# Differential attention in a hybrid encoder: one joint maximum over all keys for both softmax components, and the small VectorE operations in another order

## The chip, the cores and the metric

The kernel runs on one core of a Trainium2 chip. The metric is the device time of one execution in microseconds (us); the time before is a median of three runs. One further view, the trace, comes from a profiled execution and gives start and duration of each instruction on each engine: TensorE (PE, with its weight loads PEld), VectorE (DVE), ScalarE (ACT), GpSimd (POOL) and SyncE (SP).

## The reference, cut to what matters

Two layers; each has an input projection, two gated scans, a differential attention over 2048 positions, and an output projection. The change lies in the attention. For each of 4 heads and each block of 128 queries:

```
def block(qblk):
    s = jnp.einsum('cbhqd,cbhkd->cbhqk', qblk, k).astype(jnp.float32)   # c: 2 components, 2048 keys
    p = jax.nn.softmax(s, axis=-1)
    w = p[0] - lam * p[1]
    return jnp.einsum('bhqk,bhkv->bhqv', w.astype(v.dtype), v)
o = rms_norm(o, norm_w) * (1.0 - lambda_init)
```

The result of a block is normalised afterwards, so the kernel computes e0 - lam * (sum0 / sum1) * e1 from the exponentials and sums of the two components, and gives the square of sum0 to the norm's epsilon.

## The kernel before, in words

A layer's attention is swept in 64 units (4 heads x 16 blocks of 128 queries). A unit has four tiles of scores s0 to s3, each 128 queries x 1024 keys in two PSUM banks: s0 and s1 are the two halves of the keys for component 0, s2 and s3 for component 1. The loop over f advances one tile per step; step f works on tile `f % 4` of unit `f // 4`, and on older units at fixed lags. In what follows "position 0 to 3" is f % 4, and a prime marks the next unit (s0' follows s3).

The order on PE, DVE, ACT and POOL is written out by hand (`manual_schedule`): each engine executes its instructions in the order in which the loop's lines issue them, and only the transfers on SP are placed by a planner. In each step PE does the scores (4 matmuls), then `values` of an older unit, then `transposes` of another. DVE does the row maxima of the tile and the combination e0 + factor * e1 of half a unit at positions 0 and 2. ACT copies the transposed weights out of PSUM (`copy`), then does its exponentials (`exps`), and at position 0 also `save`, which empties the output bank `po` before `values` of the next unit may begin at position 1. At lag 1 of every eighth step ACT has one more instruction between `copy` and `exps`, `fetch`: every second unit from unit 16 to 46 PE computes at position 3 a product for the scans (`poi`, 12 matmuls ahead of s3), and `fetch` takes it out of PSUM at position 0 of the unit after.

PSUM is full: s tiles and `poi` together have three double-bank buffers, dealt out by a counter that all their allocations share, and by `acc`, which the projections call 148 times in a layer ahead of its attention. Two of three turns take one of two buffers of pool "b" (whichever is free first), the third takes the only one of pool "t":

```
        turn[0] += 1
        key, bufs = (("b", 2), ("b", 2), ("t", 1))[turn[0] % 3]
        return psum[key][1].tile([P, 2, 512], F32, tag="two", name=name, bufs=bufs)
```

A layer's attention takes 272 turns (256 s and 16 poi) and the output projection 16. Two single banks remain: one holds `po` over four steps, the other the transposed weights `pt`.

Before the change component 0 has one maximum over both halves (`mx[:, 4]`, the smaller of two negated maxima), and its two exponentials run together at position 2. Component 1 has a maximum for each half: the exponential of s2 runs at position 3 and that of s3 at position 0 of the next unit, each as soon as its own maximum is there. Two weights (`weights`, L929) and their corrections (`lows`, `total`, `factors`) bring the halves together later, so that `combine` has a factor for each half.

On POOL, the scan states (L768, L771) run beside the first units of a layer, the normalisation of the scans' output (L825 to L838) beside the middle units, and the splitting of the output weights (L785, L787) beside the later ones; the casts of queries (L723, L725) and the gates (L943, L944) run throughout.

Of the kernel before, what the change touches and what calls it, by code (L numbers as in the profile page):

```python
# [11 lines left out]
F32 = mybir.dt.float32  # L12
# [3 lines left out]
AF = mybir.ActivationFunctionType  # L16
ALU = mybir.AluOpType
AX = mybir.AxisListType
# [3 lines left out]
P = 128  # L22
# [28 lines left out]
EPS = 1e-6  # L51
# [9 lines left out]
def tile_hybrid_encoder(  # L61
# [9 lines left out]
    nc = tc.nc  # L71
# [168 lines left out]
    for l in range(DEPTH):  # L240
# [12 lines left out]
        if l == 0:  # L253
            h_st, hhi, hlo, npre = open_h(0)
            w_st, w_first = open_w(0)
# [488 lines left out]
            psum_close("s")  # L744
            psum_open("b", f"psb{l}", "left")

# [1 line left out]
        with ExitStack() as s2:  # L748
            at = at_st.enter_context(tc.tile_pool(name=f"at{l}", bufs=1, side="left"))
            si_st = ExitStack()  # L750
# [12 lines left out]
            for i in range(14):  # L763
                for d in range(2):
                    c, sh = (i + 1, 1) if d == 0 else (14 - i, -1)
# [74 lines left out]
                    nc.sync.dma_start(dr_y[self.r, 768:1024], oi[:, 256:512])  # L840

            class Unit:
                """One block of 128 queries of one head; s counts its tiles of scores (component, half of the keys)."""

                def __init__(self, i):
                    self.h, self.qb = divmod(i, NT)
                    self.j = self.qb % 2
                    if self.j == 0:
                        if (self.h, self.qb // 2) not in qs_of:
                            load_q(self.h, self.qb // 2)  # L850
                    self.qh, self.ql, self.ga = qs_of[self.h, self.qb // 2]
                    self.ks, self.v = kv[self.h]
                    self.mx = at.tile([P, 6], F32, tag="mx", name="mx", bufs=4)
                    self.sm = at.tile([P, 4], F32, tag="sm", name="sm", bufs=4)
                    self.gm = at.tile([P, 10], F32, tag="gam", name="gam", bufs=4)
                    self.s, self.pt, self.wt = [None] * 4, [None] * 4, [None] * 4

                def scores(self, k):
# [8 lines left out]
                        nc.tensor.matmul(s[:, i], self.ql[:, c, js], kk, start=False, stop=True)  # L867

                def maxima(self, k):
                    mx = self.mx  # L870
                    nc.vector.tensor_reduce(mx[:, k:k + 1], self.s[k].rearrange("p a n -> p (a n)"), axis=AX.X, op=ALU.max,  # L871
                                            negate=True)
                    if k == 1:
                        nc.vector.tensor_tensor(mx[:, 4:5], mx[:, 0:1], mx[:, 1:2], op=ALU.min)

                def exps(self, k):
                    for kk in ((), (0, 1), (2,), (3,))[k]:
                        c, n = divmod(kk, 2)
                        m = 4 if c == 0 else kk
                        nc.scalar.activation(self.es[c][:, n * 1024:(n + 1) * 1024], self.s[kk].rearrange("p a n -> p (a n)"),  # L880
                                             AF.Exp, bias=self.mx[:, m:m + 1], accum_out=self.sm[:, kk:kk + 1])

                def lows(self):
                    nc.vector.tensor_tensor(self.mx[:, 5:6], self.mx[:, 2:3], self.mx[:, 3:4], op=ALU.min)

                def sums(self):
                    gm, sm = self.gm, self.sm
                    nc.vector.tensor_tensor(gm[:, 2:3], sm[:, 0:1], sm[:, 1:2], op=ALU.add)

                def sums2(self):  # L890
                    gm = self.gm
                    nc.vector.tensor_scalar(gm[:, 1:2], gm[:, 2:3], neglam, None, op0=ALU.mult)
                    nc.vector.tensor_scalar(gm[:, 3:4], gm[:, 2:3], EPS, gm[:, 2:3], op0=ALU.mult, op1=ALU.mult)

                def total(self):
                    gm, sm = self.gm, self.sm
                    nc.vector.scalar_tensor_tensor(gm[:, 6:8], gm[:, 4:6], 1.0, sm[:, 2:4], op0=ALU.mult, op1=ALU.mult,
                                                   accum_out=gm[:, 0:1])

                def inverse(self):  # L900
                    nc.vector.reciprocal(self.gm[:, 0:1], self.gm[:, 0:1])

                def factors(self):
                    gm = self.gm
                    nc.vector.tensor_scalar(gm[:, 8:10], gm[:, 4:6], gm[:, 0:1], gm[:, 1:2], op0=ALU.mult, op1=ALU.mult)

                def combine(self, n):
                    es, gm, hs = self.es, self.gm, slice(n * 1024, (n + 1) * 1024)
                    nc.vector.scalar_tensor_tensor(es[0][:, hs], es[1][:, hs], gm[:, 8 + n:9 + n], es[0][:, hs],  # L909
                                                   op0=ALU.mult, op1=ALU.add)  # L910

                def transposes(self, q):
# [8 lines left out]
                def values(self, q):  # L921
                    if q == 0:
                        self.po = one_bank([P, P], "po", "t")
                    for i in range(4):
                        k = 4 * q + i
                        nc.tensor.matmul(self.po, self.wt[q][:, i], self.v[:, k], start=k == 0, stop=k == NT - 1)  # L926

                def weights(self):
                    nc.scalar.activation(self.gm[:, 4:6], self.mx[:, 2:4], AF.Exp, scale=-1.0, bias=self.mx[:, 5:6])  # L929

                def save(self):
                    self.o = at.tile([P, P], F32, tag="o", name="o", bufs=2)
# [16 lines left out]
            with tc.manual_schedule(engines={getattr(mybir.EngineType, e) for e in ENGINES}):  # L949
                for f in range(4 * NU + 13):  # L950
# [7 lines left out]
                    def at_lag(lag, name, k=None, *args):  # L958
                        i, m = divmod(f - lag, 4)
                        if 0 <= i < NU and k in (None, m):  # L960
                            getattr(units[i], name)(*((m,) if k is None else args))

                    def inter(lag, name):
                        c, k = divmod(f - lag - 4 * I0 - 3, 4 * I_STEP)
                        if k == 0 and 0 <= c < NT:
                            if name is None:
                                inters[c] = Inter(c)
                            else:
                                getattr(inters[c], name)()
# [3 lines left out]
                    at_lag(0, "scores")  # L973
                    at_lag(9, "values")
                    at_lag(7, "transposes")
                    at_lag(4, "lows", 0)
                    at_lag(6, "combine", 0, 0)
                    at_lag(6, "combine", 2, 1)
                    at_lag(5, "total", 0)
                    at_lag(3, "sums", 0)  # L980
                    at_lag(0, "maxima")
                    at_lag(5, "inverse", 0)
                    at_lag(3, "sums2", 0)
                    at_lag(5, "factors", 0)
                    at_lag(8, "copy")
                    inter(1, "fetch")
                    at_lag(1, "exps")
                    at_lag(4, "weights", 0)
                    at_lag(10, "norm", 3)
                    at_lag(9, "save", 3)  # L990
                    inter(2, "square")
# [129 lines left out]
```

## Time and profile before

| | |
|---|---|
| median of 3 runs | 3755.73 us |
| lowest, highest run | 3752.49, 3758.89 us |
| span of the profiled execution, first to last instruction | 3752.0 us |
| PE, PEld busy | 94%, 85% of the span |
| DVE, ACT, POOL busy | 72%, 59%, 50% of the span |
| attention of layer 0, of layer 1 | about 1034 to 1675 us, 2905 to 3550 us |

The page gives no separate time for the profiled execution; its span lies 0.5 us under the lowest run. The shares are means over stages with different limits, so the attention has to be read by its own stretches.

### The profile page before, as it was taken

The numbers are of one execution on the slowest core, as the hardware profiler recorded it, in microseconds if no ns is written. First come the engines' busy times: TensorE is split into PE (matmuls) and PEld (weight loads), VectorE is DVE, ScalarE is ACT, GpSimd is POOL, SyncE is SP. The second block draws the span as 40 slices with busy tenths as digits, with TensorE's granted clock in tenths as the row PEclk, the third lists the DMA queues.
The fourth block names the chain that finished last, engine by engine and source line by source line (L and its number), as shares of the span: only waits on it lengthen the run. The fifth ranks groups of instructions, "written<-read, shape, count | busy, mean of one in ns | idle before, by whom it ended". The sixth has DMA issues, their size and how long they took to land.

```text
span 3752.0 us, 62823 instructions
## 1 busy us (share of the span) xinstructions
PE 3534.9 (94%) x22976; PEld 3175.5 (85%) x22976; DVE 2691.2 (72%) x4122; ACT 2203.1 (59%) x5140; POOL 1868.5 (50%) x1854
## 2 busy tenths in 40 slices
PE   8999989988989999899999999999889899998999
PEld 7898978877978999788888989889779789997887
DVE  5422789988499999985324238898784999999733
ACT  4521577755568888774225125776555778887722
POOL 3545655565576666520035455555555756664200
PEclk9999999999999999999999999999999999999999
DMA  4443444444441332214334444444444413322133
GB/s 156 133 136 128 134 129 138 137 123 135 131 136 33 117 119 85 66 32 133 120 115 150 125 127 136 129 137 140 126 126 132 126 39 117 115 79 66 38 134 114
DMA packets 293652, 430.54 MB, mean 115 GB/s; under 512 B 42400, under 2 KB 185312, under 8 KB 291040
## 3 DMA queue, kind: packets, MB, share of 16 engines
q1 hardware_dynamic: 268896, 333.71, 28.7%
q0 software_dynamic: 22336, 90.71, 8.3%
q8 instruction: 182, 2.98, 0.3%
q10 hardware_dynamic: 2112, 2.10, 0.2%
q14 instruction: 126, 1.03, 0.1%
HBM read 275.82 MB, written 152.57 MB: 114 GB/s over the span
## 4 chain that ended last, share of the span: by engine, by line
PE 51%; DVE 27%; DMA 10%; issue 4%; POOL 4%; ACT 3%; SPq 1%; DVEq 0%; POOLq 0%; ACTq 0%
PE pp L306 11%; PE pob L1031 9%; PE po L926 8%; PE pp L297 6%; DVE mx L871 5%; PE s L866 4%; PE s L867 4%; PE pt L915 4%; DMA wraw<-in_w_in_dram 3%; DVE e L909 3%; DVE qt L612 3%; DVE pr L545 3%; DVE att L605 2%; DMA cs<-c_rope 2%; PE poi L816 1%
## 5 line engine op out<-in xcount | busy, mean ns | idle before, releaser
L880 ACT ACTIVATE e<-s,mx 128x1024 f32<-128x1024 f32 x512 | 570.5, 1118 | 146.6 <-DVE mx L871 107.3
L871 DVE TENSOR_REDUCE mx<-s 128x1 f32<-128x1024 f32 x512 | 621.3, 1215 | 36.7 <-PE s L867 35.9
L306 PE MATMUL pp<-wlo,hhi 128*128 128x256 f32 (+1 forms) x2048 | 591.0, 289 | 7.8 <-POOL wlo L224 7.7
L926 PEld LDWEIGHTS po<-vt,wt 128*128 128x128 f32 x4096 | 533.2, 191 | 70.0 <-ACT o L933 30.0
L306 PE MATMUL pp<-whi,hlo 128*128 128x256 f32 (+1 forms) x2048 | 591.8, 289 | 0.1
L306 PE MATMUL pp<-whi,hhi 128*128 128x256 f32 (+1 forms) x2048 | 588.0, 287 | 3.0 <-DVE whi L223 3.0
L926 PE MATMUL po<-vt,wt 128*128 128x128 f32 x4096 | 544.1, 276 | 17.4 <-ACT o L933 17.4
L866 PE MATMUL s<-ks,aqh 128*128 128x512 f32 x1024 | 449.7, 439 | 28.0 <-ACT e L880 26.5
L297 PE MATMUL pp<-hhi,whi 128*128 128x512 f32 x1024 | 412.1, 402 | 3.7 <-DVE zg L428 2.4
L297 PE MATMUL pp<-hhi,wlo 128*128 128x512 f32 x1024 | 410.1, 400 | 0.0
L297 PE MATMUL pp<-hlo,whi 128*128 128x512 f32 x1024 | 410.0, 400 | 0.0
L867 PE MATMUL s<-ks,aql 128*128 128x512 f32 x1024 | 404.0, 395 | 5.2 <-POOL aql L725 5.2
L306 PEld LDWEIGHTS pp<-wlo,hhi 128*128 128x128 f32 x2048 | 393.1, 192 | 8.8 <-POOL wlo L224 8.8
L306 PEld LDWEIGHTS pp<-whi,hhi 128*128 128x128 f32 x2048 | 395.0, 193 | 4.1 <-DVE whi L223 3.8
L306 PEld LDWEIGHTS pp<-whi,hlo 128*128 128x128 f32 x2048 | 393.8, 192 | 0.7 <-DVE hlo L195 0.3
L909 DVE SCALAR_TENSOR_TENSOR e<-e,gam 128x1024 f32<-128x1024 f32 x256 | 367.1, 1434 | 4.5
L919 ACT COPY wt<-pt 128x512 f32<-128x512 f32 x512 | 300.5, 587 | 100.1 <-PE pt L915 98.3
L915 PE MATMUL pt<-ident,e 128*128 128x128 f32 x2048 | 310.5, 274 | 14.5 <-DVE e L909 8.7
L610 POOL TENSOR_TENSOR kt<-kt,nt 128x512 f32<-128x512 f32 x144 | 191.7, 1334 | 206.0 <-DVE kl L588 106.7
L915 PEld LDWEIGHTS pt<-ident,e 128*128 128x128 f32 x2048 | 238.7, 141 | 23.3 <-ACT wt L919 11.3
L866 PEld LDWEIGHTS s<-ks,aqh 128*128 128x128 f32 x1024 | 194.4, 190 | 61.3 <-ACT e L880 36.5
L214 POOL DMA_DIRECT2D wraw<-in_w_in_dram x124 | 97.4, 786 | 283.0 <-DVE sso L1038 183.8
(198 smaller groups left out, 8165.7 us busy)
## 6 DMA issues: line engine op xcount, KB each, us to landing
wraw<-in_w_in_dram POOLq DMA_DIRECT2D x116, 512.0 KB, 4.8
cs<-c_rope SPq DMA_DIRECT2D x32, 512.0 KB
dr_gate<-z SPq DMA_DIRECT2D x64, 256.0 KB
aq<-dr_q SPq DMA_DIRECT2D x256, 64.0 KB
ks<-dr_k POOLq DMA_DIRECT2D x16, 1024.0 KB, 8.1
y<-dr_y SPq DMA_DIRECT2D x32, 512.0 KB
dr_qs<-qt SPq DMA_DIRECT2D x48, 256.0 KB
qs<-dr_qs SPq DMA_DIRECT2D x24, 512.0 KB
```

The costliest lines, as they stand in the source:

```text
L297: nc.tensor.matmul(ps.rearrange("p (a t) -> p a t", t=P), w[a][:, k, c:c + P], b[g][:, :, k], start=n == 0, stop=n == 3 * KC - 1)
L306: nc.tensor.matmul(ps, b[g][:, t % 4, k], w[a][:, k, :n], start=cnt == 0, stop=cnt == 3 * KC - 1)
L610: nc.gpsimd.tensor_tensor(ka, ka, custom(tt, toff + 1, [(tn - 1, 2), (2, n2), (0, h)]), op=ALU.mult)
L866: nc.tensor.matmul(s[:, i], self.qh[:, c, js], kk, start=True, stop=False)
L867: nc.tensor.matmul(s[:, i], self.ql[:, c, js], kk, start=False, stop=True)
L871: nc.vector.tensor_reduce(mx[:, k:k + 1], self.s[k].rearrange("p a n -> p (a n)"), axis=AX.X, op=ALU.max, negate=True)
L880: nc.scalar.activation(self.es[c][:, n * 1024:(n + 1) * 1024], self.s[kk].rearrange("p a n -> p (a n)"), AF.Exp, bias=self.mx[:, m:m + 1], ...
L909: nc.vector.scalar_tensor_tensor(es[0][:, hs], es[1][:, hs], gm[:, 8 + n:9 + n], es[0][:, hs], op0=ALU.mult, op1=ALU.add)
L915: nc.tensor.transpose(pt[:, i], self.es[0][:, (4 * q + i) * P:(4 * q + i + 1) * P], ident)
L919: nc.scalar.copy(wt, self.pt[q])
L926: nc.tensor.matmul(self.po, self.wt[q][:, i], self.v[:, k], start=k == 0, stop=k == NT - 1)
L1031: nc.tensor.matmul(pos[:, n], a[:, k], b[k][:, n * 512:(n + 1) * 512], start=cnt == 0, stop=cnt == 3 * KC - 1)
```

## The change: what it does

Both components get one maximum over all 2048 keys (`joint`). The two exponentials of component 0 still run at position 2; those of component 1 now both run at position 0 of the next unit, after the maximum of s3. With equal offsets no weights are needed: `lows`, `weights`, `total`, `sums2` and `factors` go. One `sums` adds the halves of both components, `inverse` is the reciprocal of the second sum, `factor` a single column, `floor` the squared sum for the norm. On DVE the order of a step changes as well: `inverse` runs ahead of the maxima of position 2, `factor` and `floor` behind them, and the combination of position 2 comes last instead of first.

```
                 def maxima(self, k):
+                    nc.vector.tensor_reduce(self.mx[:, k:k + 1], self.s[k].rearrange("p a n -> p (a n)"), axis=AX.X, op=ALU.max,
+                                            negate=True)
+                def joint(self, c):
                     mx = self.mx
-                    nc.vector.tensor_reduce(mx[:, k:k + 1], self.s[k].rearrange("p a n -> p (a n)"), axis=AX.X, op=ALU.max,
-                                            negate=True)
-                    if k == 1:
-                        nc.vector.tensor_tensor(mx[:, 4:5], mx[:, 0:1], mx[:, 1:2], op=ALU.min)
-                def exps(self, k):
-                    for kk in ((), (0, 1), (2,), (3,))[k]:
-                        c, n = divmod(kk, 2)
-                        m = 4 if c == 0 else kk
-                        nc.scalar.activation(self.es[c][:, n * 1024:(n + 1) * 1024], self.s[kk].rearrange("p a n -> p (a n)"),
-                                             AF.Exp, bias=self.mx[:, m:m + 1], accum_out=self.sm[:, kk:kk + 1])
-                def lows(self):
-                    nc.vector.tensor_tensor(self.mx[:, 5:6], self.mx[:, 2:3], self.mx[:, 3:4], op=ALU.min)
+                    nc.vector.tensor_tensor(mx[:, 4 + c:5 + c], mx[:, 2 * c:2 * c + 1], mx[:, 2 * c + 1:2 * c + 2], op=ALU.min)
+                def exps(self, c):
+                    for n in range(2):
+                        nc.scalar.activation(self.es[c][:, n * 1024:(n + 1) * 1024],
+                                             self.s[2 * c + n].rearrange("p a n -> p (a n)"), AF.Exp,
+                                             bias=self.mx[:, 4 + c:5 + c], accum_out=self.sm[:, n, c:c + 1])
                 def sums(self):
-                    nc.vector.tensor_tensor(gm[:, 2:3], sm[:, 0:1], sm[:, 1:2], op=ALU.add)
-                def sums2(self):
-                    nc.vector.tensor_scalar(gm[:, 1:2], gm[:, 2:3], neglam, None, op0=ALU.mult)
-                    nc.vector.tensor_scalar(gm[:, 3:4], gm[:, 2:3], EPS, gm[:, 2:3], op0=ALU.mult, op1=ALU.mult)
-                def total(self):
-                    nc.vector.scalar_tensor_tensor(gm[:, 6:8], gm[:, 4:6], 1.0, sm[:, 2:4], op0=ALU.mult, op1=ALU.mult,
-                                                   accum_out=gm[:, 0:1])
+                    nc.vector.tensor_tensor(self.gm[:, 0:2], self.sm[:, 0], self.sm[:, 1], op=ALU.add)
                 def inverse(self):
-                    nc.vector.reciprocal(self.gm[:, 0:1], self.gm[:, 0:1])
+                    nc.vector.reciprocal(self.gm[:, 2:3], self.gm[:, 1:2])
-                def factors(self):
-                    nc.vector.tensor_scalar(gm[:, 8:10], gm[:, 4:6], gm[:, 0:1], gm[:, 1:2], op0=ALU.mult, op1=ALU.mult)
+                def floor(self):
+                    nc.vector.tensor_scalar(gm[:, 3:4], gm[:, 0:1], EPS, gm[:, 0:1], op0=ALU.mult, op1=ALU.mult)
+                def factor(self):
+                    nc.vector.scalar_tensor_tensor(gm[:, 4:5], gm[:, 0:1], neglam, gm[:, 2:3], op0=ALU.mult, op1=ALU.mult)
-                def weights(self):
-                    nc.scalar.activation(self.gm[:, 4:6], self.mx[:, 2:4], AF.Exp, scale=-1.0, bias=self.mx[:, 5:6])
...
                     at_lag(7, "transposes")
-                    at_lag(4, "lows", 0)
+                    at_lag(6, "inverse", 0)
+                    at_lag(6, "combine", 2, 1)
+                    at_lag(0, "maxima")
+                    at_lag(0, "joint", 1, 0)
+                    at_lag(0, "joint", 3, 1)
+                    at_lag(5, "sums", 0)
+                    at_lag(6, "factor", 0)
+                    at_lag(6, "floor", 0)
                     at_lag(6, "combine", 0, 0)
-                    at_lag(6, "combine", 2, 1)
-                    at_lag(5, "total", 0)
-                    at_lag(3, "sums", 0)
-                    at_lag(0, "maxima")
-                    at_lag(5, "inverse", 0)
-                    at_lag(3, "sums2", 0)
-                    at_lag(5, "factors", 0)
                     at_lag(8, "copy")
                     inter(1, "fetch")
-                    at_lag(1, "exps")
-                    at_lag(4, "weights", 0)
+                    at_lag(1, "exps", 1, 0)
+                    at_lag(1, "exps", 3, 1)
```

## Rows read from the trace of the kernel before

**Rows 1.** Busy time by stretch: us, then PE, PEld, DVE, ACT, POOL, PEclk, DMA, GB/s.

```profile
1060.00:1200.00 140.00, 126.07 (x843) 110.84 (x843) 137.16 (x199) 104.01 (x240) 107.48 (x96) 0.99 0.23 71
1200.00:1500.00 300.00, 299.81 (x2153) 277.12 (x2152) 284.60 (x458) 251.79 (x597) 184.22 (x249) 1.00 0.33 103
1500.00:1640.00 140.00, 127.63 (x873) 112.79 (x871) 137.26 (x204) 105.71 (x249) 64.42 (x66) 1.00 0.18 58
...
2925.00:3075.00 150.00, 136.92 (x920) 121.08 (x919) 145.40 (x216) 111.60 (x255) 110.95 (x101) 0.98 0.25 73
3075.00:3370.00 295.00, 293.76 (x2105) 271.27 (x2103) 279.65 (x451) 247.63 (x587) 181.84 (x246) 1.00 0.33 104
3370.00:3510.00 140.00, 127.62 (x872) 112.80 (x871) 137.14 (x204) 105.82 (x248) 66.01 (x68) 1.00 0.18 58
```

**Rows 2.** Groups on DVE by shape, 1075 to 1200 us: busy, mean ns.

```profile
L871 DVE TENSOR_REDUCE mx<-s 128x1 f32<-128x1024 f32 x47 | 56.9, 1212 | 1.4 <-PE s L867 1.4
L909 DVE SCALAR_TENSOR_TENSOR e<-e,gam 128x1024 f32<-128x1024 f32 x24 | 38.5, 1602 | 0.4
L905 DVE TENSOR_SCALAR gam<-gam 128x2 f32<-128x2 f32 x12 | 9.3, 771 | 0.4
...
L884 DVE TENSOR_TENSOR mx<-mx 128x1 f32<-128x1 f32 x12 | 5.5, 462 | 0.0
...
L897 DVE SCALAR_TENSOR_TENSOR gam<-gam,sm 128x2 f32<-128x2 f32 x12 | 4.9, 411 | 0.0
L892 DVE TENSOR_SCALAR gam<-gam,neglam 128x1 f32<-128x1 f32 x12 | 2.4, 198 | 0.0
```

**Rows 3.** Timeline of a pair of units, layer 0, ACT: start us, duration us.

```profile
1303.94 1.11 ACT L880 ACTIVATE e<-s,mx 128x1024 f32<-128x1024 f32 x1 [0.86 <-DVE mx L871]
...
1305.99 0.59 ACT L821 COPY sq<-poi 128x512 f32<-128x512 f32 x1
1306.47 1.13 ACT L880 ACTIVATE e<-s,mx 128x1024 f32<-128x1024 f32 x1
...
1307.57 0.30 ACT L929 ACTIVATE gam<-mx 128x2 f32<-128x2 f32 x1
1307.76 0.27 ACT L933 COPY o<-po 128x128 f32<-128x128 f32 x1
...
1315.18 1.12 ACT L880 ACTIVATE e<-s,mx 128x1024 f32<-128x1024 f32 x1
...
1316.46 0.26 ACT L933 COPY o<-po 128x128 f32<-128x128 f32 x1
```

**Rows 4.** Timeline of the same pair, PE (matmuls) and DVE.

```profile
1304.13 1.23 DVE L871 TENSOR_REDUCE mx<-s 128x1 f32<-128x1024 f32 x1 [0.16 <-PE s L867]
...
1305.20 0.49 PE L866 MATMUL s<-ks,aqh 128*128 128x512 f32 x1
...
1314.23 0.48 PE L866 MATMUL s<-ks,aqh 128*128 128x512 f32 x1
...
1317.49 1.05 PE L926 MATMUL po<-vt,wt 128*128 128x128 f32 x8
```

**Rows 5.** Two releases of PE by ACT, at 1122 us and at 1577 us.

```profile
1122.28 1.11 ACT L880 ACTIVATE e<-s,mx 128x1024 f32<-128x1024 f32 x1 [1.57 <-DVE mx L874]
...
1123.53 0.50 PE L866 MATMUL s<-ks,aqh 128*128 128x512 f32 x1 [1.19 <-ACT e L880]
...
1577.45 0.27 ACT L933 COPY o<-po 128x128 f32<-128x128 f32 x1
...
1577.77 1.16 PE L926 MATMUL po<-vt,wt 128*128 128x128 f32 x8
...
1579.90 0.40 PE L867 MATMUL s<-ks,aql 128*128 128x512 f32 x1
```

**Rows 6.** Timeline of DVE alone, 1575 to 1581 us.

```profile
1575.98 1.28 DVE L909 SCALAR_TENSOR_TENSOR e<-e,gam 128x1024 f32<-128x1024 f32 x1
...
1578.31 0.15 DVE L897 SCALAR_TENSOR_TENSOR gam<-gam,sm 128x2 f32<-128x2 f32 x1
```

More of the change, by code (lines that the diff above doesn't have):

```diff
@@ L853, in __init__ @@
                     self.mx = at.tile([P, 6], F32, tag="mx", name="mx", bufs=4)
-                    self.sm = at.tile([P, 4], F32, tag="sm", name="sm", bufs=4)
-                    self.gm = at.tile([P, 10], F32, tag="gam", name="gam", bufs=4)
+                    self.sm = at.tile([P, 2, 2], F32, tag="sm", name="sm", bufs=4)
+                    self.gm = at.tile([P, 5], F32, tag="gam", name="gam", bufs=4)
                     self.s, self.pt, self.wt = [None] * 4, [None] * 4, [None] * 4
@@ L886, in sums @@
+                def exps(self, c):
[3 more added lines that the diff above has]
+                                             bias=self.mx[:, 4 + c:5 + c], accum_out=self.sm[:, n, c:c + 1])
                 def sums(self):
-                    gm, sm = self.gm, self.sm
-                    nc.vector.tensor_tensor(gm[:, 2:3], sm[:, 0:1], sm[:, 1:2], op=ALU.add)
@@ L890, in sums2, with inverse @@
-                def sums2(self):
+                    nc.vector.tensor_tensor(self.gm[:, 0:2], self.sm[:, 0], self.sm[:, 1], op=ALU.add)
+                def inverse(self):
+                    nc.vector.reciprocal(self.gm[:, 2:3], self.gm[:, 1:2])
+                def floor(self):
                     gm = self.gm
-                    nc.vector.tensor_scalar(gm[:, 1:2], gm[:, 2:3], neglam, None, op0=ALU.mult)
-                    nc.vector.tensor_scalar(gm[:, 3:4], gm[:, 2:3], EPS, gm[:, 2:3], op0=ALU.mult, op1=ALU.mult)
@@ L895, in total @@
-                def total(self):
-                    gm, sm = self.gm, self.sm
-                    nc.vector.scalar_tensor_tensor(gm[:, 6:8], gm[:, 4:6], 1.0, sm[:, 2:4], op0=ALU.mult, op1=ALU.mult,
-                                                   accum_out=gm[:, 0:1])
-                def inverse(self):
-                    nc.vector.reciprocal(self.gm[:, 0:1], self.gm[:, 0:1])
-                def factors(self):
+                    nc.vector.tensor_scalar(gm[:, 3:4], gm[:, 0:1], EPS, gm[:, 0:1], op0=ALU.mult, op1=ALU.mult)
@@ L904, in factors @@
+                def factor(self):
                     gm = self.gm
-                    nc.vector.tensor_scalar(gm[:, 8:10], gm[:, 4:6], gm[:, 0:1], gm[:, 1:2], op0=ALU.mult, op1=ALU.mult)
+                    nc.vector.scalar_tensor_tensor(gm[:, 4:5], gm[:, 0:1], neglam, gm[:, 2:3], op0=ALU.mult, op1=ALU.mult)
                 def combine(self, n):
-                    es, gm, hs = self.es, self.gm, slice(n * 1024, (n + 1) * 1024)
-                    nc.vector.scalar_tensor_tensor(es[0][:, hs], es[1][:, hs], gm[:, 8 + n:9 + n], es[0][:, hs],
+                    es, hs = self.es, slice(n * 1024, (n + 1) * 1024)
+                    nc.vector.scalar_tensor_tensor(es[0][:, hs], es[1][:, hs], self.gm[:, 4:5], es[0][:, hs],
```

## The prediction

> **What bounds the kernel now.** I read the page first: PE is busy 94% of the span, but that mean joins stages with different limits, so next I cut the attention into stretches [rows 1]. Each layer shows the same three. In the middle one (units 16 to 46, with the scans' products) PE is busy 299.8 of 300 us: here PE alone sets the time, and whatever stops PE is paid in full. In the stretches before and after it DVE is busy 97 to 98% and PE idles: 13.9, 12.4, 13.1 and 12.4 us, 51.8 in all. Those are the stretches where a lighter DVE can pay, and 51.8 us is all that it can give, as PE's work stays.
>
> Why DVE is full there is seen in its groups by shape [rows 2]: operations on one or two columns take 0.4 to 0.8 us, while L892 on one column takes 0.198. The long ones are held up by POOL, which is busy 107 of 140 us there. Then I read one pair of units in the middle stretch on ACT and PE [rows 3, 4] for the slack of each wait, since a change that moves exponentials changes when PSUM buffers come free.
>
> **The change part by part.**
>
> *What DVE saves.* Per unit it has six small operations instead of eight, none of them with an accumulator read. At 0.2 us each, as L892 has it [rows 2], that is 0.4 us a unit, and it counts only in the outer stretches. Being held: above their unheld 0.15 to 0.29, and 1.28 for a combination, the rows give 0.32 for each `combine`, 0.48 for L905, 0.31 for a `joint`-like L884, 0.26 for L897 [rows 2]; with L888 and L874 like L884, some 2.3 us per unit over seven operations that can be held. After the change six remain.
>
> One might price the new `factor` like L892, 0.2 us, and so win all of L905's 0.77. L897 is the same operation on two columns, and its mean is 0.41, so I price it like that [rows 2]. The Trainium skill (SBUF — State Buffer, section "Who interferes with whom") says the same and speaks against this edit: a VectorE operation with two inputs in SBUF waits for a GpSimd instruction that reads SBUF, as one in a two-port mode does. The trace agrees as far as it goes (0.771 for L905, 0.198 for L892). By the rule a hold moves from L905 to `factor` or `combine`; without it the outer stretches would gain about 0.4 us a unit more, some 18 us over 44 units.
>
> *A new loop through ACT.* The exponential of s2 no longer runs at position 3 but behind `joint`, ahead of that of s3. `save` stood behind one exponential and `weights` at position 0; now it stands behind two. PE's `values` at position 1 waits for `save`, and s2' is queued behind it. From `joint` on: exponential to exponential 1.10 us (1306.47 to 1307.57, where `weights` begins), the second 1.10, `save` 0.27 and 0.05 to PE; from there to the end of s2' 2.53 us (1577.77 to 1580.30) [rows 3, 5]; then on DVE a maximum and `combine` (2.33 from start to start [rows 6]), `factor` and `floor` between them, a maximum and `joint`: 2.33 + 0.25 + 1.21 + 0.2 = 4.0. The loop is 9.1 us a unit, whereas PE alone needs 9.0 for a unit without `poi` (1305.20 to 1314.23) [rows 4]. In the outer stretches a unit now takes 125 us / (47/4 maxima) = 10.6 us [rows 2]. There three of the held operations lie on the loop (`factor`, `combine`, `joint`), about 1.0 us: 10.1, plus something because several waits must all end. I take a gain of 0.3 us on 44 units, 13 us, less 2 us for the units at the end where POOL is quiet and PE already runs at 9.0: 11 us. Bounds: nothing, and 51.8.
>
> *What PE loses in the middle stretch.* Three buffers hold the score tiles and `poi`. In a unit with `poi`, the tile after s3 must find one while `poi` and s3 hold two; the third is that of s2. Before, s2 was read at position 3 (exponential at 1303.94), done at 1305.2 with its accumulator read, just when PE began s0' at 1305.20 [rows 3, 4]: it fits without a wait, and with no slack. After, s2 is read at position 0: ACT does the `copy`, `fetch` (1305.99), and only then has room, at 1306.47. `joint` is no later: the maximum of s3 begins at 1304.13 and takes 1.23. An exponential that starts at 1122.28 frees its tile for PE at 1123.53, 1.25 us later [rows 5]. So s0' starts at 1307.72 instead of 1305.20: PE stands 2.5 us, in a stretch where it has no idle time.
>
> Whether s0' must have just that buffer follows from the counter. Layer 0: 148 turns before, so attention's n-th tile takes pool "t" when n mod 3 is 1. In unit 16 s2 is the 67th, `poi` the 68th, s0' the 70th: s2 and s0' both take the single buffer of "t", and as a pair takes 9 turns this repeats 16 times. Layer 1: 148 + 288 + 148 turns, "t" when n mod 3 is 0; s2, `poi` and s0' all take "b". There s0' may take `poi`'s buffer, which `fetch` frees ahead of the exponential: 1305.99 + 0.59 + 0.05 = 1306.63, a stand of 1.4 us. Bounds in layer 1: 1.4 and 2.5.
>
> The second unit of the pair waits at `save`: it ended at 1316.72, and PE's `values` began at 1317.49 [rows 3, 4]. Afterwards 1315.18 + 2 x 1.10 + 0.26 + 0.05 = 1317.69; behind a wait PE's weight loads no longer run ahead, so I take 0.3 us. A late `combine` at position 2 (now behind a maximum, with `factor` that can be held) can delay `transposes` at position 3. I take 0.1, bounds 0 and 0.3, a mean hold [rows 2]. Together per pair 2.9 us in layer 0 and 1.8 in layer 1; 16 pairs each: 47 + 29 = 76 us.
>
> *Nothing.* `weights` gone (0.19 us of ACT) is inside the sum above. The buffers of e, mx, sm, gm are four each and are still free two units later; no transfer is moved, and SP and POOL keep their order. `save` a microsecond later delays POOL's gating, which waits for ACT already and has a unit's time until the gate's buffer is wanted.
>
> *Sum.* 76 - 11 = +65 us. On the span of 3752.0 us that is 3817; the lowest run is 0.5 us above this span and the median 3.7 above it, which gives 3817.5 to 3820.7. I predict 3820 us.
>
> **The rivals.**
>
> *Both layers wait for the exponential.* If in layer 1 s0' gets s2's buffer as well, its pairs cost 2.9: 16 x 1.1 = 17 us more, 3838. For it: in the layout of before s0' takes over s2's buffer whenever `poi`'s is still held. Against: `fetch` stands ahead of the exponential on ACT.
>
> *Faster.* DVE is the limit of the outer stretches and the change takes work off it; if the loop through `save` is not what binds there, because `copy` and `save` find gaps, they fall to PE's pace and give up to 51.8 us, of which I count 45. This decides only if PE's new wait in the middle costs less: that needs s0' to take a buffer that is free already, so that only the wait at `save` is left, 32 x 0.3 = 10 us. Then 3755.7 - 45 + 10 = 3721. Against it stands the order of ACT's rows. The Trainium skill (VectorE: DVE Perf Modes, section "Rules for kernel authors") would have it so: for chained VectorE operations the number of operations is to be kept low, and here it falls. No run shows it yet; in the outer stretches the trace gives the condition, in the middle one VectorE isn't the limit.
>
> *Full relief, but the stand stays.* 2.5 x 16 + 1.4 x 16 = 62 us, less 45: 3773.
>
> *No measurable change.* Stand and relief cancel: the stand is 1.4 in both layers and relief 45, about 3756.
>
> **How the numbers follow.** Forecast (3820) 0.55; both layers 0.20; full relief with the stand 0.09; cancel 0.05; faster 0.06; more than these, if PE's idle spells cost granted clock or second waits grow, 0.05. A difference of 0.2% (7.5 us) is about what a measurement of this kernel can tell from no change. Faster 0.06, same 0.05, slower 0.89. The range takes in full relief below (3773) and above both layers without any relief, 3838 + 11: 3772 to 3850, which leaves the faster and the cancelling case and the last one outside. The forecast's own range is 3800 to 3832.
>
> **What would show it.** In the middle stretch of layer 0 PE waits for ACT's exponential (L866 on `exps`) 16 times for about 2.5 us, against almost never now, and PE is no longer at 100%; a pair of units takes 2.9 us longer. In layer 1 the same wait is about 1.4 us, or on `fetch`. `values` waits for `save` more often in all stretches. In the outer stretches DVE's share falls below 97%, as DVE now waits for s2'. Wrong would be: no wait of L866 in the middle; or outer stretches that shrink by more than 20 us a layer; or a granted clock below 1.00 in the middle stretch.

## The result, and the profile after

The changed kernel takes 3846.42 us (median of 4 runs, 3844.20 to 3848.50) against 3754.11 for the kernel before beside it: ratio 1.0241, interval 1.0226 to 1.0255. It is 92 us slower. Its profiled span is 3846.7 us, 94.7 more than before; the accounts below are made against that.

First the stretches of [rows 1] but the last, cut at the first and last unit with `poi`: us, then PE, PEld, DVE, ACT, POOL busy, PEclk, DMA share, GB/s.

```profile
1060.00:1200.00 140.00, 124.89 (x840) 110.16 (x839) 128.67 (x160) 99.69 (x225) 107.81 (x98) 0.99 0.25 74
1200.00:1590.00 390.00, 352.72 (x2338) 319.86 (x2336) 271.18 (x401) 268.62 (x618) 178.46 (x266) 0.94 0.27 83
1590.00:1690.00 100.00, 90.08 (x608) 78.49 (x607) 88.08 (x116) 71.82 (x163) 50.32 (x46) 1.00 0.21 65
2980.00:3130.00 150.00, 131.11 (x860) 113.26 (x860) 134.82 (x170) 104.74 (x228) 111.31 (x99) 0.99 0.33 88
3130.00:3470.00 340.00, 320.39 (x2259) 289.87 (x2259) 261.18 (x389) 260.69 (x600) 174.79 (x261) 1.00 0.30 91
```

PE is no longer busy throughout in either middle stretch: it idles 37 of 390 us in layer 0 and 20 of 340 in layer 1. In layer 0 its granted clock is 0.94 as well, where [rows 1] had 1.00. In the outer stretches DVE has fallen from 97-98% to 88-92%, yet PE idles as much as before: 15.1 us of 140 in the first, where it was 13.9.

What PE and its weight loads wait for in the middle of layer 0 (view of waits, 1212 to 1590 us: total us, times, longest):

```profile
PEld s L866 <- ACT e L879: 41.1, 16, 2.6
...
PE s L866 <- ACT e L879: 37.3, 16, 2.4
...
PEld po L916 <- ACT o L920: 4.6, 16, 0.3
```

The same view in the middle of layer 1 (3140 to 3465 us):

```profile
PEld s L866 <- ACT sq L821: 23.3, 16, 1.5
...
PEld po L916 <- ACT o L920: 5.1, 15, 0.4
```

Sixteen waits each, one per pair of units: the weight loads of s0' stand 2.57 us in layer 0, for the exponential, and 1.46 us in layer 1, for `fetch`. The forecast had 2.5 and 1.4, with those two releasers. The weight loads of `values` wait 0.3 us for `save`, as forecast. PE's matmuls idle a little less, 37.3 us in layer 0 and 19.6 in layer 1, all of it at s0' and none at `values`.

One of these stands in layer 0, on PE's matmuls (start us, duration us):

```profile
1327.81 1.05 PE L916 MATMUL po<-vt,wt 128*128 128x128 f32 x8
1328.70 0.60 PE L905 MATMUL pt<-ident,e 128*128 128x128 f32 x4
1331.63 0.50 PE L866 MATMUL s<-ks,aqh 128*128 128x512 f32 x1 [2.33 <-ACT e L879]
...
1332.28 0.63 PE L866 MATMUL s<-ks,aqh 128*128 128x512 f32 x1
...
1333.13 1.91 PE L916 MATMUL po<-vt,wt 128*128 128x128 f32 x8
1334.83 0.93 PE L905 MATMUL pt<-ident,e 128*128 128x128 f32 x4
```

And on ACT:

```profile
1329.39 0.59 ACT L909 COPY wt<-pt 128x512 f32<-128x512 f32 x1 [2.65 <-PE pt L905]
1329.88 0.59 ACT L821 COPY sq<-poi 128x512 f32<-128x512 f32 x1
1330.35 1.13 ACT L879 ACTIVATE e<-s,mx 128x1024 f32<-128x1024 f32 x1
...
1331.46 1.13 ACT L879 ACTIVATE e<-s,mx 128x1024 f32<-128x1024 f32 x1
```

The order is the one forecast: `copy`, `fetch`, the exponential of s2 at 1330.35, and PE starts s0' 1.28 us after that. What the forecast's sum did not have stands in the PE rows after the wait: eight `values` matmuls take 1.91 us instead of 1.05, four transposes 0.93 instead of 0.60. By windows (columns as above), before this stand, right behind it and later in the pair:

```profile
1326.50:1328.00 1.50, 1.50 (x11) 1.32 (x11) 0.97 (x1) 0.24 (x1) 0.00 (x0) 1.00 0.44 133
1332.10:1335.40 3.30, 3.30 (x15) 3.00 (x14) 1.22 (x1) 0.84 (x3) 2.83 (x7) 0.50 0.00 0
1336.00:1354.00 18.00, 17.01 (x123) 15.40 (x122) 14.55 (x23) 13.31 (x32) 5.78 (x8) 1.00 0.25 74
```

PE is busy in all 3.3 us of the second window, and granted half its clock (1.2 of 2.4 GHz). The trace has such a spell, 3.4 us long, behind 14 of the 16 stands in layer 0 and none in the middle of layer 1. Its price is half of 14 x 3.4 us, 24 us; the second row of the stretches gives much the same, 0.06 of 390 us. That is some 1.5 us a pair.

The cost of the middle stretch can be read from where PE starts the first scores of unit 16 and of unit 48; between them lie the 16 pairs. Layer 0, then layer 1, before:

```profile
1196.91 0.47 PE L866 MATMUL s<-ks,aqh 128*128 128x512 f32 x1
1509.60 0.48 PE L866 MATMUL s<-ks,aqh 128*128 128x512 f32 x1
...
3064.08 0.47 PE L866 MATMUL s<-ks,aqh 128*128 128x512 f32 x1
3377.89 0.48 PE L866 MATMUL s<-ks,aqh 128*128 128x512 f32 x1
```

and after:

```profile
1201.50 0.48 PE L866 MATMUL s<-ks,aqh 128*128 128x512 f32 x1
1577.68 0.48 PE L866 MATMUL s<-ks,aqh 128*128 128x512 f32 x1
...
3136.38 0.47 PE L866 MATMUL s<-ks,aqh 128*128 128x512 f32 x1
3473.44 0.47 PE L866 MATMUL s<-ks,aqh 128*128 128x512 f32 x1
```

A pair took 19.5 us and takes 23.5 in layer 0 (4.0 more); in layer 1 it took 19.6 and takes 21.1 (1.5 more). So 63.5 + 23.3 = 87 us of the 94.7 come from the middle stretches. Counted in the same way, units 0 to 15 and 48 to 63 of both layers together are 2.7 us longer than before, and everything outside the attention is 5.2 us longer. The outer stretches give nothing back.

Why not, with DVE lighter? DVE's groups by shape in the first outer stretch of layer 0 (1075 to 1200 us, as [rows 2]: busy, mean ns, idle before):

```profile
L870 DVE TENSOR_REDUCE mx<-s 128x1 f32<-128x1024 f32 x48 | 58.1, 1216 | 7.5 <-PE s L867 7.4
L899 DVE SCALAR_TENSOR_TENSOR e<-e,gam 128x1024 f32<-128x1024 f32 x25 | 44.1, 1766 | 0.0
L895 DVE SCALAR_TENSOR_TENSOR gam<-gam,neglam 128x1 f32<-128x1 f32 x12 | 8.5, 705 | 0.0
...
L891 DVE TENSOR_SCALAR gam<-gam 128x1 f32<-128x1 f32 x12 | 2.4, 202 | 0.0
```

DVE now waits for PE's scores (7.4 us). PE waits for `combine`, as the view of who waited for that line shows; after:

```profile
  PE pt L905: 43.4, 36
```

and before, for L909:

```profile
  PE pt L915: 8.7, 16
```

All of the 43.4 us lie in the outer stretches. In exchange PE waits less there for the exponentials and for `save`: over units 0 to 15 and 48 to 63 of both layers it idles 64.0 us in all, where it idled 63.5.

`combine` of position 2 now stands behind a maximum, `factor` and `floor`; the `transposes` at position 3 need it. On DVE that reads, at 1150 us:

```profile
1149.06 1.23 DVE L870 TENSOR_REDUCE mx<-s 128x1 f32<-128x1024 f32 x1 [0.56 <-PE s L867]
1150.20 0.29 DVE L895 SCALAR_TENSOR_TENSOR gam<-gam,neglam 128x1 f32<-128x1 f32 x1
1150.41 0.20 DVE L891 TENSOR_SCALAR gam<-gam 128x1 f32<-128x1 f32 x1
1150.54 2.38 DVE L899 SCALAR_TENSOR_TENSOR e<-e,gam 128x1024 f32<-128x1024 f32 x1
```

and on PE:

```profile
1153.06 0.63 PE L905 MATMUL pt<-ident,e 128*128 128x128 f32 x4 [0.90 <-DVE e L899]
```

Here `combine` itself was slow as well: it took 2.38 us, where its median over the run is 1.28.

### The profile page after: what moved, and what is told of

Read it like the earlier page. It is cut to its first block, busy times and chain, and to the rows that moved or that the text cites. A ratio compares the mean times of both kernels' runs of the same rounds, so it can differ in the third digit from the quotient of the medians.

```text
span 3846.7 us, 62335 instructions
## 1 busy us (share of the span) xinstructions
PE 3571.1 (93%) x22976; PEld 3191.8 (83%) x22976; DVE 2564.0 (67%) x3738; ACT 2176.3 (57%) x5012; POOL 1833.9 (48%) x1854
## 4 chain that ended last, share of the span: by engine, by line
PE 61%; DVE 19%; DMA 8%; issue 4%; ACT 4%; POOL 3%; SPq 1%; DVEq 0%; ACTq 0%; POOLq 0%
PE pp L306 11%; PE po L916 11%; PE pob L1018 9%; PE pp L297 9%; PE s L866 6%; PE pt L905 6%; PE s L867 5%; DMA wraw<-in_w_in_dram 3%; DVE qt L612 2%; DVE pr L545 2%; DVE att L605 2%; DVE e L899 2%; DVE mx L870 2%; DMA cs<-c_rope 1%; ACT e L879 1%
## 5 line engine op out<-in xcount | busy, mean ns | idle before, releaser
L916 PEld LDWEIGHTS po<-vt,wt 128*128 128x128 f32 x4096 | 541.1, 195 | 73.3 <-ACT o L920 36.6
L916 PE MATMUL po<-vt,wt 128*128 128x128 f32 x4096 | 561.6, 281 | 4.5 <-ACT o L920 3.4
L909 ACT COPY wt<-pt 128x512 f32<-128x512 f32 x512 | 303.2, 592 | 318.8 <-PE pt L905 318.8
L905 PE MATMUL pt<-ident,e 128*128 128x128 f32 x2048 | 315.5, 278 | 43.5 <-DVE e L899 43.4
L899 DVE SCALAR_TENSOR_TENSOR e<-e,gam 128x1024 f32<-128x1024 f32 x256 | 354.2, 1384 | 0.0
L905 PEld LDWEIGHTS pt<-ident,e 128*128 128x128 f32 x2048 | 243.9, 144 | 50.7 <-issue 48.4
L297 PEld LDWEIGHTS pp<-hhi,whi 128*128 128x128 f32 x1024 | 196.6, 192 | 46.2 <-DVE zg L428 2.8
```

The lines of the kernel that those rows point to most:

```text
L297: nc.tensor.matmul(ps.rearrange("p (a t) -> p a t", t=P), w[a][:, k, c:c + P], b[g][:, :, k], start=n == 0, stop=n == 3 * KC - 1)
L899: nc.vector.scalar_tensor_tensor(es[0][:, hs], es[1][:, hs], self.gm[:, 4:5], es[0][:, hs], op0=ALU.mult, op1=ALU.add)
L905: nc.tensor.transpose(pt[:, i], self.es[0][:, (4 * q + i) * P:(4 * q + i + 1) * P], ident)
L909: nc.scalar.copy(wt, self.pt[q])
```

## The experiments

The theory after the result: the loss is the late exponential of s2, which stops PE for 2.5 us where the PSUM buffers are dealt as in layer 0 and for 1.5 us where they are dealt as in layer 1, and a stand of 2.5 us costs clock besides; the outer stretches gain nothing because `combine` comes last. The rivals: the loss is the new order of DVE and not the exponential; the layers differ by something other than the dealing; fewer small operations are worth nothing anyway.

**e1_turn: layer 0 dealt as layer 1.** The counter of the PSUM turns is set ahead of each layer's attention. Layer 1's attention is dealt as it was; layer 0's output projection, which takes its turns from the same counter, is dealt otherwise too.

```
+            turn[0] = 2
             with tc.manual_schedule(engines={getattr(mybir.EngineType, e) for e in ENGINES}):
```

> The changed kernel, with the buffer counter set to 2 ahead of each layer's attention: layer 0 is then dealt as layer 1 is (s2, poi and s0' all from pool b), layer 1 as it was. Theory (PE stands for the buffer of s2 in layer 0, and after a stand of 2.5 us its granted clock is halved for a spell): layer 0's pairs fall from 4.4 us over the time before to 1.6, 16 x 2.8 = 45 us less, about 3801; L866 waits on fetch, no longer on the exponential, and the clock in the middle stretch of layer 0 is 1.00. Rival 1 (the halved clock costs nothing, other work hides it): only the shorter stand counts, 16 x 1.1 = 18 us, about 3828. Rival 2 (it is the order on ACT, not the buffer): no change, 3846.

Measured: 3802.07 us, 1.0126 (1.0109 to 1.0143), 44 us less than the changed kernel. Its waits in the middle of layer 0 (1212 to 1540 us) are those of layer 1:

```profile
PEld s L866 <- ACT sq L821: 23.4, 16, 1.5
```

and its window there has the full clock:

```profile
1212.00:1540.00 328.00, 308.43 (x2175) 279.31 (x2175) 252.73 (x374) 252.31 (x577) 173.37 (x258) 1.00 0.30 94
```

Units 16 to 47 of layer 0 take 337.1 us, 39 less than in the changed kernel. The shorter stand explains 16 x (2.57 - 1.46) = 18 of them; the other 21 go with the clock. The remaining 5 of the 44 lie elsewhere, where the traces scatter by several us. Who gets which buffer is thus a lever of its own, and a free one.

**e2_turn_l1: layer 1 dealt as layer 0.** The same line with 4.

```
+            turn[0] = 4
             with tc.manual_schedule(engines={getattr(mybir.EngineType, e) for e in ENGINES}):
```

> The changed kernel, with the counter set to 4 ahead of each layer's attention: layer 1 is then dealt as layer 0 is (s2 and s0' share the one buffer of pool t). Theory: layer 1 gets the stand of 2.5 us and the halved clock that layer 0 has, 45 us more, about 3891. Rival 1 (clock free of cost): 18 us more, 3864. Rival 2 (order on ACT): 3846.

Measured: 3885.80 us, 1.0349 (1.0333 to 1.0364): 39 us more than the changed kernel, of which 18 are the longer stand; units 16 to 47 of layer 1 take 40 us more. In layer 1 the waits (3140 to 3500 us) and the window are now:

```profile
PEld s L866 <- ACT e L879: 38.5, 15, 2.6
```

```profile
3150.00:3510.00 360.00, 325.16 (x2141) 295.65 (x2141) 245.44 (x366) 244.49 (x564) 168.79 (x255) 0.93 0.28 85
```

With e1 this makes the dealing the cause of the difference between the layers: moved either way, wait, releaser and clock go with it.

**e3_late: the late exponential alone, on the kernel before.** s2's exponential moves behind s3's maximum; weights, corrections and DVE's order stay.

```
-                    for kk in ((), (0, 1), (2,), (3,))[k]:
+                    for kk in ((), (0, 1), (), (2, 3))[k]:
```

> The kernel before, with one edit: the exponential of s2 runs at position 0, directly ahead of that of s3, as after the change; maxima for each half, weights, corrections and the order on DVE stay. Theory (the lateness of this one instruction is the whole loss): the stands come as in the changed kernel, 3754 + 96 = 3850, or a few us more for weights and its eight small operations. Rival (the new order of the small operations is a good part of the loss, in the outer stretches): below 3835.

Measured: 3862.82 us, 1.0289 (1.0273 to 1.0304). One index table makes the whole loss and 16 us more. Its waits in layer 0 (1212 to 1600 us) have the row of the changed kernel, under its own line number:

```profile
PEld s L866 <- ACT e L880: 41.1, 16, 2.6
```

**e4_early: the change with the exponentials of component 1 early again.** Each half uses its own maximum, and the corrections that this would need are left out, so that only six small operations remain.

```
...
-                    at_lag(1, "exps", 1, 0)
-                    at_lag(1, "exps", 3, 1)
+                    at_lag(1, "exps")
```

> The changed kernel, with one edit: the exponentials of component 1 use the maximum of their own half and run at position 3 and 0, as before; the corrections for the different offsets are left out, so the two halves are not weighted against each other. Joint maxima are still computed. Theory: without the late exponential no stand is left, and what remains is what the fewer small operations and their new order do alone: between 3703 (all of PE's idle time in the outer stretches) and 3754. Rival (the small operations or their order cost time themselves): above 3765.

Measured: 3772.21 us, 1.0052 (1.0036 to 1.0068). The theory fell here: I expected no loss to be left, and 18 us are, as the rival had it. PE idles 9 of 300 us in the middle, where it idled 0.2 before:

```profile
1200.00:1500.00 300.00, 290.92 (x2084) 267.99 (x2083) 263.30 (x359) 241.08 (x548) 177.01 (x245) 1.00 0.33 101
```

The place is the one seen above in the outer stretches. On DVE and on PE's weight loads, once a pair:

```profile
1334.12 0.94 DVE L897 SCALAR_TENSOR_TENSOR gam<-gam,neglam 128x1 f32<-128x1 f32 x1
...
1335.11 1.43 DVE L901 SCALAR_TENSOR_TENSOR e<-e,gam 128x1024 f32<-128x1024 f32 x1
...
1336.65 0.42 PEld L907 LDWEIGHTS pt<-ident,e 128*128 128x128 f32 x4 [0.76 <-ACT lnv L164]
```

The profile puts the 0.76 us down to an instruction of ACT, but the transposes read e, and e's writer ends at 1336.54, just ahead. `combine`, behind a maximum and a held `factor`, is late.

**e5_spaced: DVE's new order alone, on the kernel before.** All eight small operations, in the order of the changed kernel.

```
                     at_lag(4, "lows", 0)
-                    at_lag(6, "combine", 0, 0)
+                    at_lag(6, "inverse", 0)
                     at_lag(6, "combine", 2, 1)
+                    at_lag(0, "maxima")
                     at_lag(5, "total", 0)
                     at_lag(3, "sums", 0)
-                    at_lag(0, "maxima")
-                    at_lag(5, "inverse", 0)
                     at_lag(3, "sums2", 0)
-                    at_lag(5, "factors", 0)
+                    at_lag(6, "factors", 0)
+                    at_lag(6, "combine", 0, 0)
```

> The kernel before, with its own eight small operations and early exponentials, but in the changed kernel's order on DVE: inverse ahead of the maximum of position 2, factors behind it, the combination of position 2 last. Theory (the combination behind the maximum makes transposes at position 3 late, 0.76 us once a pair in the middle stretch and more where POOL holds factors): 15 to 30 us slower than before, 3770 to 3785, with waits of transposes. Rival (spacing dependent operations apart saves their stalls; the 18 us in the run with early exponentials came from the fewer operations in some other way): at or below 3754.

Measured: 3784.47 us, 1.0069 (1.0042 to 1.0097). The order alone costs 0.7%, with nothing else changed. That settles what e4 had opened. The cost lies in the middle stretches, 14.0 us in layer 0 and 12.9 in layer 1 (units 16 to 47); the outer ones change by 2.7 us at most.

**e10_early_first: e4 with `combine` first again.** `factor`, `floor` and `combine` go ahead of the maximum of position 2, and `inverse` runs a step earlier; as in e4 the corrections are left out. The diff is against e4.

```
-                    at_lag(6, "inverse", 0)
+                    at_lag(6, "factor", 0)
+                    at_lag(6, "floor", 0)
+                    at_lag(6, "combine", 0, 0)
                     at_lag(6, "combine", 2, 1)
                     at_lag(0, "maxima")
...
                     at_lag(5, "sums", 0)
-                    at_lag(6, "factor", 0)
-                    at_lag(6, "floor", 0)
-                    at_lag(6, "combine", 0, 0)
+                    at_lag(5, "inverse", 0)
```

> The changed kernel's six small operations with the early exponentials of before (uncorrected offsets, so the two halves of component 1 are not weighted against each other) and with factor, floor and the combination of position 2 ahead of that position's maximum, as the combination stood before. Theory: this is what the fewer operations give when neither the late exponential nor the late combination takes it back: the outer stretches gain 5 to 10 us each, 3715 to 3735. Rival (fewer small operations give nothing, the holds by POOL only move): 3750 to 3758.

Measured: 3729.63 us, 0.9932 (0.9919 to 0.9944). Fewer small operations (and no `weights` on ACT) are worth some 25 us when nothing takes them back; 21 of them lie in the outer stretches, 16 in units 48 to 63. In the last outer stretch of layer 0 PE has 134.40 us of work in 140, where [rows 1] has 127.63; in the middle it is full:

```profile
1200.00:1500.00 300.00, 300.00 (x2155) 277.38 (x2155) 266.89 (x372) 249.59 (x569) 195.05 (x252) 1.00 0.34 103
1500.00:1640.00 140.00, 134.40 (x928) 120.75 (x928) 136.21 (x173) 110.54 (x249) 64.98 (x65) 1.00 0.19 60
```

**e9_combine_first: the same order in the changed kernel, exponentials late.** The diff on the changed kernel is the one shown for e10.

> The changed kernel, with one edit: factor, floor and the combination of position 2 run ahead of that position's maximum, as the combination did before, and inverse runs one position earlier; late exponentials stay. Theory (the order took back in the outer stretches what the fewer operations gave): the middle stretch keeps its stands, the outer ones gain some 5 us each, 3825 to 3835. Rival (the loop through save binds in the outer stretches whatever the order): 3842 to 3850.

Measured: 3838.22 us, 1.0217 (1.0194 to 1.0241), between theory and rival; its interval overlaps that of the changed kernel (1.0226 to 1.0255), so a gain of some 8 us is likely but not certain. By stretch it is plain: units 48 to 63 are 6 us shorter in each layer than in the changed kernel, units 0 to 15 differ by 1.2 and -2.5, and units 16 to 47 of layer 1 are 6 us longer. Over the whole span the wait of `transposes` falls from 48.4 to 3.9 us, while that of the scores for the exponential rises from 67.0 in 40 waits to 90.2 in 64. In the first outer stretches the late exponential was the second limit behind `combine`; with one gone, the other binds. In the last ones PE's idle time falls, from 9.9 to 5.3 us in layer 0.

**e6_fill: work for PE during the wait.** At position 0 PE does `values` and `transposes` ahead of the scores.

```
-                    at_lag(0, "scores")
+                    if f % 4:
+                        at_lag(0, "scores")
                     at_lag(9, "values")
                     at_lag(7, "transposes")
+                    if f % 4 == 0:
+                        at_lag(0, "scores")
```

> The changed kernel, with one edit on PE: at position 0 values and transposes run ahead of the scores, so that PE has work while it waits for the buffer of s2. Theory (stand and halved clock are PE's idle time at that wait): the stand of 2.5 us shrinks by about 1.1, the clock stays at 1.00, layer 0 loses 2.7 us a pair less, layer 1 1.1 to 1.4: 43 + 20 less, about 3783. Rival (s0' and its maximum now come 1.1 us later in every unit and DVE, ACT and save follow): above 3830.

Measured: 3790.30 us, 1.0095 (1.0072 to 1.0119), 56 us less than the changed kernel. The stand in layer 0 is halved (waits, 1215 to 1530 us), and the clock stays up:

```profile
PEld s L866 <- ACT e L879: 18.9, 16, 1.3
```

```profile
1215.00:1530.00 315.00, 299.94 (x2117) 271.43 (x2116) 243.76 (x363) 241.38 (x560) 166.08 (x248) 1.00 0.32 97
```

Units 16 to 47 are 43 us shorter in layer 0, as expected, but only 9 in layer 1, where 20 were expected. There the weight loads of `values` now wait for `save` in nearly every unit (15.2 us in 31 waits, 3100 to 3420 us) and PE hardly idles; what keeps the other 11 us was not taken apart.

**e7_fetch_last: `fetch` behind both exponentials.** s2's buffer comes free earlier, that of `poi` later.

```
-                    inter(1, "fetch")
                     at_lag(1, "exps", 1, 0)
                     at_lag(1, "exps", 3, 1)
+                    inter(1, "fetch")
```

> The changed kernel, with one edit on ACT: fetch runs behind both exponentials instead of ahead of them. The stand is then 2.5 - 0.48 = 2.0 us in both layers, as poi's buffer comes free last. Theory: if a stand of 2.0 us halves the clock as 2.5 does, layer 0 gains 8 and layer 1 loses 16 x (0.6 + 1.6) = 35, about 3873; if it does not, layer 0 gains 8 + 26 and layer 1 loses 10, about 3822. Rival (layer 1 is not bound by the buffers): 3838, layer 0's 8 us alone.

Measured: 3872.00 us, 1.0310 (1.0288 to 1.0333). The time is the expected one, but not for the expected reason alone. Both layers wait for the exponential, 2.07 us each time (layer 1, 3140 to 3500 us):

```profile
PEld s L866 <- ACT e L879: 33.2, 16, 2.1
```

The clock, though, falls only behind 6 of 16 stands in layer 0 and 7 in layer 1 (0.97 in both stretches), not behind all. The other part is a wait of `transposes` that the changed kernel doesn't have in the middle: 8.3 us in 10 waits in layer 0 (1212 to 1569 us), 7.4 in 9 in layer 1. By units 16 to 47, layer 0 gains 10 us and layer 1 loses 30; the remaining 6 of the 26 us lie elsewhere. So `fetch` ahead of the exponentials is the better order for the kernel as it is dealt, and the worse one for layer 0 alone.

**e8_half: the shift from the first half alone.** The maxima of s1 and s3 and the joint maxima are left out: each component is shifted by the maximum of its first 1024 keys, so the guard against far larger scores in the second half is gone. Each exponential runs one position behind its scores, `combine` comes first, `factor` and `floor` run a step early.

```
...
-                                             bias=self.mx[:, 4 + c:5 + c], accum_out=self.sm[:, n, c:c + 1])
+                                         bias=self.mx[:, 2 * c:2 * c + 1], accum_out=self.sm[:, n, c:c + 1])
...
-                    at_lag(0, "maxima")
-                    at_lag(0, "joint", 1, 0)
-                    at_lag(0, "joint", 3, 1)
+                    if f % 2 == 0:
+                        at_lag(0, "maxima")
...
-                    at_lag(1, "exps", 1, 0)
-                    at_lag(1, "exps", 3, 1)
+                    at_lag(1, "exps")
```

> A version that takes the shift for both halves of a component from the maximum of its first half alone: softmax does not depend on the shift, so nothing has to be corrected, and the maxima of s1 and s3 and both joint maxima are left out. (The shift then no longer guards against a score in the second half that lies some 88 above every score of the first; these inputs have none.) Each tile's exponential runs one position after its scores; the combination of position 2 runs ahead of the maximum, factor and floor at position 1. Theory: no stand in the middle stretch, and DVE loses 2.3 us of two maxima a unit, so the outer stretches fall to PE's pace: 3754 less 40 to 52, 3702 to 3715. Rival (the outer stretches are bound by the way through ACT and save): 3735 to 3754.

Measured: 3690.05 us, 0.9826 (0.9813 to 0.9840), faster than both kernels and than expected. PE never idles from the middle of layer 0 to the end of these stretches:

```profile
1060.00:1200.00 140.00, 129.41 (x897) 118.50 (x896) 92.33 (x109) 106.86 (x235) 113.83 (x102) 0.98 0.27 79
1200.00:1500.00 300.00, 300.00 (x2169) 278.59 (x2168) 204.79 (x250) 250.63 (x576) 204.31 (x258) 1.00 0.33 102
1500.00:1640.00 140.00, 140.00 (x997) 129.34 (x996) 94.05 (x125) 120.00 (x266) 64.42 (x62) 1.00 0.19 60
```

## Why the prediction was right, and where its terms were off

**Right: the stand.** Its place, its releaser in each layer, its count and its size came out as worked out, 2.57 for 2.5 and 1.46 for 1.4 us, and the layers differ by the dealing of three buffers (e1, e2). The 0.3 us at `save` came out as a wait of the weight loads, but PE's matmuls don't idle there. The rival in which both layers wait for the exponential was not this kernel; e2 shows its time, 3886 and not 3838, since the stand brings the clock with it and the outer stretches give nothing.

**Mis-sized: "2.9 us in layer 0".** The term counted the stand and left the granted clock at 1.00. The prediction named the clock twice, as a case of 0.05 that it left outside its range and as a sign that it would be wrong, but put no price into the sum. That sign came true in layer 0. Measured, layer 0 pays 63.5 us instead of 47: PE idles 37 us at s0' and loses 24 by the clock. Layer 1 pays 23.3 instead of 29, of which 19.6 are idle time at s0'. The Trainium skill (TensorE: Matmul & The Clock Gate, section "A second HAM failure mode: psum-queue depth-cycling") tells of a kernel whose short idle spells between groups of matmuls, as it cycled through PSUM, sent the clock to and fro; this trace agrees (16 stands, 0.94 in that stretch).

**Failed: "11 us" from the outer stretches.** They came out 2.7 us longer. The step that failed is the late `combine`: "I take 0.1" was priced for the middle stretch alone, and in the outer ones `combine` is counted in DVE's own loop but not as a wait of PE's `transposes`. There PE waits 43.4 us for it, 34.7 more than before, while its other waits shrink by as much. By stretch, in us against the kernel before (L0, L1: layers; units counted from the starts of their scores, as above):

| run | L0 0-15 | L0 16-47 | L0 48-63 | L1 0-15 | L1 16-47 | L1 48-63 | elsewhere |
|---|---|---|---|---|---|---|---|
| changed | +2.5 | +63.5 | -1.8 | +3.8 | +23.3 | -1.8 | +5.2 |
| e4 | -2.6 | +10.0 | +0.8 | -2.5 | +9.0 | +1.0 | -0.1 |
| e5 | -1.3 | +14.0 | +2.7 | -1.0 | +12.9 | +2.4 | +3.4 |
| e9 | +3.7 | +63.4 | -8.0 | +1.4 | +29.5 | -7.6 | +0.2 |
| e10 | -2.6 | -1.1 | -8.1 | -2.8 | -2.3 | -7.8 | -1.2 |

Each row is one trace, and "elsewhere" scatters by several us. In units 48 to 63 fewer operations are worth 8 us a layer as long as `combine` is early (e9, e10); the late `combine` takes some 6 of them (changed) to 9 (e4). In units 0 to 15 they are worth some 2.6 (e4, e10), whatever the place of `combine`, and the late exponential takes that and more (changed, e9). With `combine` early the outer stretches of e9 give 10.5 us, the forecast's 11, but by luck: all of it lies in units 48 to 63, for the end of which the forecast took 2 us off, and none in the first units. The 0.7% that the order costs with early exponentials (e5) lies in the middle stretches, so it is not what the outer ones lost.

**Right in kind: the hold moves.** `factor` took 0.705 us, near L905's 0.771, and not the 0.41 that was priced; `floor`, on one column, took 0.202. The Trainium skill (SBUF — State Buffer, section "Who interferes with whom") has it that an operation with two inputs in SBUF contends with POOL's reads; the trace agrees with these two rows. The mean of `combine` rose as well, from 1.602 to 1.766 us.

**Faster and cancelling rivals.** They needed the outer stretches to fall to PE's pace while the middle costs little. Neither holds with late exponentials. With them early and `combine` first part of the relief is there, 21 us of the 45 counted (e10). The bound of 51.8 was too low: [rows 1] begin 26 us behind the first scores of layer 0, over all outer units PE idled 63.5 us, and e8 took 58 out of them. The rule of the Trainium skill (VectorE: DVE Perf Modes, section "Rules for kernel authors") that the number of chained operations should be kept low is borne out by e10, not by the change.

The account by stretch closes: 63.5 + 23.3 + 2.7 + 5.2 = 94.7 us on the span, against 47 + 29 - 11 = 65 forecast. The time lies in the range given (3772 to 3850), beyond the forecast's own (3800 to 3832). That it lies in the range is luck: the upper end was set for both layers at 2.9 us a pair without any relief, and the clock, which took the room kept for layer 1, was left out of it. What is not settled: why 2 of the 16 stands of 2.57 us cost no clock, and which part of e8's further gain comes from fewer maxima and which from earlier exponentials.

## What to carry to other kernels

Where PE is full and PSUM has no spare buffer, an operation that reads PSUM later can stop PE for its whole delay each time the next tile needs just that buffer (here once in a pair of units); work out which allocation takes over which buffer before moving it, since that alone was worth 44 us here. Count the granted clock with every stand of PE that comes back regularly: here it added more than half as much again to a stand of 2.5 us. And when operations are taken off a busy engine, keep the one that the next engine waits for at the head of the step, or the relief goes into waiting.

## What the runs showed of the hardware that was not expected

A stand of 2.57 us, once in a pair of 23.5 us in which PE is otherwise busy, is followed by 3.4 us at half the clock (14 of 16 pairs; 0.50 in the window shown). Stands of 1.46 us (layer 1, e1) and of 1.18 us (e6) are not; stands of 2.07 us (e7) are in 13 of 32 pairs. An operation on DVE can be late by being held once: the same `factor` took 0.29 us at 1150.20 in the changed kernel and 0.94 at 1334.12 in e4. And the releaser that the profile names for a wait of several semaphores can be another engine's (ACT for the 0.76 us in e4); the writer of the tile that the waiting instruction reads is the surer guide.
